# A two-block decoder kernel: square sums and half of the weight sums by accumulating DMA, and weights in order of use

## The chip, the cores and the metric

The kernel runs on one core of one Trainium2 chip. The metric is the device time of one execution in microseconds; the kernel before has a median of 2129.83 us over 3 runs (2126.9 to 2134.0). The engines are TensorE (PE, matrix products), VectorE (DVE), ScalarE (ACT) and GpSimd (POOL); SyncE (SP) issues nearly all DMAs. Each engine works through its own instructions in order and waits for others by semaphores.

## The reference

512 tokens of width 1024 (with 16 more meta tokens in the first block) go through two blocks in fp32. Around the change, each block ends or begins with a feed-forward (FFN) of width 2816:

```python
def rms_norm(x, g):
    y = xf * lax.rsqrt(jnp.mean(xf * xf, axis=-1, keepdims=True) + EPS)
    return y * g
# first block: mixers, then
h = h + m @ w_o
hn = rms_norm(h, norm2_g)
gate, up = jnp.split(hn @ w_gate_up, 2, axis=-1)
x = rms_norm(h + (silu(gate) * up) @ w_down, final_g)
# second block
x = x + 0.5 * swiglu(rms_norm(x, ffn1_norm), ffn1_w_gate, ffn1_w_up, ffn1_w_down)
...   # two attentions with gates g_fox, g_sb
merged = sigmoid(g_fox) * (y_fox @ w_branch_fox) + sigmoid(g_sb) * (y_sb @ w_branch_sb)
x = x + merged @ w_out
x = x + 0.5 * swiglu(rms_norm(x, ffn2_norm), ffn2_w_gate, ffn2_w_up, ffn2_w_down)
x = x + sigmoid(rms_norm(x, ple_norm) @ w_ple_gate) * (p @ w_ple_proj)
```

## The kernel before

Activations lie transposed: 128 features by 512 tokens to a tile, 8 tiles to the width. Every fp32 operand is split into a high part (ACT's cast, `wh`, `zm`, `hh`) and a low part (DVE's difference in `low`, L374), and a product is three matmuls.

In the order of time the stages are: the first block's mixers (to 482 us), its `w_o` (to 527), the first FFN (to 883), the second FFN (to 1267), the second block's mixers (to 1625), its branch product and `w_out` (to 1704), the third FFN (to 2070), and the last gate. At the turn from one to the next stands a *border*: the first is ahead of the first FFN, the second ahead of the second FFN, the third ahead of the third FFN.

An FFN has 22 pairs of 128 gate and 128 up columns, in three parts of 6, 8 and 8 pairs (`CHUNKS`, L1322). A pair is computed by seven products in place of eight (class `Pair`, class `Gated`, `p1` to `p8`), each of 12 matmuls with 256 columns. Its weights come in four pieces `a`, `b`, `c`, `d`; half of piece `a` is a sum of two parts of the up weights (L1113), half of `c` a sum of gate and up parts (L1117), others are differences (L1118, L1120), all on DVE. Each piece is then cast (L1142) and its low half taken. There are 5 buffers for raw pieces and 6 for split ones. After a part's pairs its hidden tiles go through the down weights (`onto`): 8 outputs `o`, in the order 0, 4, 1, 5, 2, 6, 3, 7 (`PAIRED`), each 512 columns wide. `Gated.tail` multiplies gate by the norm factor `rv`, takes silu and multiplies with up; in a down output DVE multiplies by `rv` and scale (L1369) and adds to the residual (L1370), two operations.

Where a stage ends, `normed.post` gets each output. ACT squares it (L940) and POOL adds the square into `ss` (L941); outputs o and o+4 make a quad, whose gains DVE multiplies in (L984, L991), whose three sums POOL takes (L996 to L998, on DVE for the last quad), and which is split into `zm`, the next FFN's operand, by ACT and DVE. So three quads are ready before the last, and the first two pairs start with five products over these three quarters (`early`) before they need the fourth. The mean of the squares is a matmul (L469); `root` computes `rv` with ACT and DVE, and p8 of the first pair cannot start until gate and up of the next are combined behind it (L1292). Ahead of the second FFN there are two statistics (`between`), since the first block's final norm and the next norm are taken together; `rest` then scales the residual by `final_g` (L1439), eight operations among the next pairs.

Inside `ordered()` the order on ACT, DVE and POOL is as recorded. Work beside the products is a task with a planned time: `tick` advances the plan by 358 ns per four-matmul step, and a due task records its next operations then. `feed` lets a task take raw and split buffers in turn and issue the weight loads on SP's queue; `wdma` (L370) is the load.

In the second block, `block2` first loads the residual that was spilled to HBM (L1666, 2 MB), then per output two tiles of gates (L1672, L1673), multiplies, and splits `m` on POOL (L422).

Of the kernel before, what the change touches and what calls it, by code (L numbers as in the profile page):

```python
# [13 lines left out]
S = 512  # L14
# [35 lines left out]
class Net:  # L50
# [3 lines left out]
    def __init__(self, ctx, tc, a):  # L54
# [20 lines left out]
            "ffn": dict(tmp=6, quad=3, x=4, raw2=2, wh2=3, wl2=3, rbc=2, aux=2),  # L75
# [851 lines left out]
    class Stats:  # L927
# [5 lines left out]
        def add(self, x, scale=1.0, eng=None):  # L933
# [12 lines left out]
    def normed(self, gains, more=(), mixed=True):  # L946
# [4 lines left out]
        class Norm:  # L951
# [7 lines left out]
            def post(n, o, x):  # L959
# [9 lines left out]
                elif o < 3:  # L969
                    n.first(o)  # L970
                elif o >= 4:
                    if o == 7:
                        n.first(3)
                    n.second(o - 4, last)
                n.stats[0].add(x)
                for st, f in zip(n.stats[1:], more):
                    st.add(x, f(o))
                if last and mixed:
                    n.task = net.task((n.make or n.root)(), 5500)

            def first(n, k):
                t = net.quad()
                n.mixes.append(t)
                net.nc.vector.tensor_scalar(t[:, 0:2].rearrange("p h c -> p (h c)"), n.res[k], gains(k), None,  # L984
                                            ALU.mult)

            def second(n, k, last):
# [3 lines left out]
                nc.vector.tensor_scalar(b[:, 2:4].rearrange("p h c -> p (h c)"), n.res[k + 4], gains(k + 4), None,  # L991
                                        ALU.mult)

                def sums(eng):
                    t = net.quad()
                    eng.tensor_tensor(t[:, 0:2], b[:, 1:3], b[:, 0:1].broadcast_to([128, 2, HT]), ALU.subtract)  # L996
                    eng.tensor_tensor(t[:, 2], b[:, 2], t[:, 0], ALU.add)  # L997
                    eng.tensor_tensor(t[:, 3], t[:, 2], b[:, 3], ALU.subtract)  # L998
                    return t
                if last:  # L1000
                    nc.scalar.copy(z[:, 0, 0:3], b[:, 1:4])
                    t = sums(nc.vector)
# [5 lines left out]
                def go():  # L1008
                    nc.scalar.copy(z[:, 0, 0:3], b[:, 1:4])
                    t = sums(nc.gpsimd)  # L1010
                    yield 1000
                    net.low(z[:, 1, 0:3], b[:, 1:4], z[:, 0, 0:3])
                    yield 1800
                    nc.scalar.copy(z[:, 0, 3:7], t)
                    yield 1200
# [38 lines left out]
    LAND = 5000  # L1054

    class Tile_:
# [16 lines left out]
        def ready(self, net):  # L1073
            net.fetched(self)
            net.need(lambda: self.ok, *net.splits(self))
            return self.w

        def done(self, net):
            net.leave(self.w)

    class Pair:
# [4 lines left out]
        def __init__(self, one, two):  # L1086
            self.one, self.two = one, two
            self.task, self.t = None, {}

        def fetch(self, net):  # L1090
            def load(to, src, k0):
                net.wdma(to, src[0], src[1], 128, k0, 4)
# [10 lines left out]
            yield from net.take("raw")  # L1103
            self.c = net.get("raw")
# [3 lines left out]
            self.at = net.now  # L1108

        def split_(self, net):  # L1110
            nc = net.nc
            a, x, y = self.a, self.x, self.y
            nc.vector.tensor_tensor(a[:, 4:8], x, y, ALU.add)  # L1113
            yield 700
            yield lambda: self.c is not None
            b, c = self.b, self.c
            nc.vector.tensor_tensor(c[:, 4:8], a[:, 0:4], x, ALU.add)  # L1117
            yield from net.split(self, 0, a, also=lambda: nc.vector.scalar_tensor_tensor(  # L1118
                b[:, 0:4], a[:, 4:8], -1.0, a[:, 0:4], ALU.mult, ALU.subtract))
            yield from net.split(self, 1, b, also=lambda: nc.vector.tensor_tensor(  # L1120
                c[:, 0:4], b[:, 4:8], b[:, 0:4], ALU.subtract))
            yield from net.split(self, 2, c)
            yield lambda: self.d is not None
            yield max(0, self.at + net.LAND - net.now)
            yield from net.split(self, 3, self.d)

        def part(self, net, p):
            net.fetched(self)
            net.need(lambda: p in self.t, *net.splits(self))
            return self.t[p]  # L1130

        def done(self, net, p):
            net.leave(self.t[p])

    def split(self, item, p, raw, single=None, also=None):

        nc = self.nc
        yield lambda: self.items[0] is item
        yield from self.take("w")
        w = self.get("wh", raw.shape[1]), self.get("wl", raw.shape[1])  # L1140
        self.order.append(w)
# [5 lines left out]
        self.give("raw")  # L1147
# [4 lines left out]
        if single or p == 3:  # L1152
            self.items.pop(0)

    def splits(self, item):
        return [x.task for x in self.items[:self.items.index(item) + 1]] + [self.fetch] if item in self.items else []

    def take(self, kind):
        while not self.free[kind]:
            yield lambda: self.free[kind] > 0  # L1160
        self.free[kind] -= 1

    def give(self, kind):
        self.free[kind] += 1

    def leave(self, w):

        self.left.append(w)
        while self.order and any(x is self.order[0] for x in self.left):
            self.order.pop(0)  # L1170
            self.give("w")

    def get(self, tag, nk=KD):

        n = self.WEIGHTS[tag], self.n[tag + "2"]
        self.at[tag] = (self.at.get(tag, -1) + 1) % sum(n)
# [580 lines left out]
```

## Time and profile before

| | |
|---|---|
| median of 3 runs | 2129.83 us (2126.9 to 2134.0) |
| profiled execution | 2130.05 us, span of its trace 2128.1 us |
| mean granted clock of TensorE | 0.979 of full |
| PE / DVE / ACT / POOL busy | 96% / 73% / 48% / 19% |
| DMA | 217.08 MB, 102 GB/s over the span |

Idle time of an engine that is not the bottleneck costs nothing. PE is the busiest, and it is not idle evenly: a table of busy time by stage shows where. At an idle stretch of PE the chain of waits tells what was late: each of its rows is the piece of work that released the next one. "lg L469" is the matmul for a mean, "r", "q" and "s" are the banks of a pair's products, "acc" the outputs of ordinary products. The granted clock is the share of TensorE's full speed (2.4 GHz) that the chip allowed.

### The profile page before, as it was taken

How to read it: one execution, taken by the hardware profiler on the slowest of the kernel's cores; microseconds unless marked ns; L12 is line 12 of the kernel's file. 1: busy time of each engine (PE TensorE's matmuls, PEld its weight loads, DVE VectorE, ACT ScalarE, POOL GpSimd, SP SyncE). 2: the span in 40 equal slices, each digit the busy share in tenths (PEclk: the TensorE clock that was granted, in tenths of full speed). 3: DMA queues.
4: the chain of work that ended last, by engine and by line, in shares of the span. 5: the costliest groups of instructions: out<-in, count | busy, mean ns of one | idle time of the engine just before them, and what ended most of it. 6: DMA issues, size and time to landing. Idle time of an engine off the chain costs nothing.

```text
span 2128.1 us, 30817 instructions
## 1 busy us (share of the span) xinstructions
PE 2032.6 (96%) x11886; PEld 1772.0 (83%) x11886; DVE 1552.1 (73%) x2428; ACT 1022.7 (48%) x1669; POOL 407.3 (19%) x245
## 2 busy tenths in 40 slices
PE   7999999999899999889999999998989989999998
PEld 6788887887889899688989977776777778999987
DVE  5889565547979787897977756666763787977854
ACT  5445554444535345453534537764543453544532
POOL 2333434004000000600000053543333410000010
PEclk9999999999999999889999999999999999999999
DMA  4221222334334435133443432331225534443413
GB/s 114 82 78 45 81 79 80 109 108 135 109 110 129 130 105 149 45 97 112 129 129 100 115 99 81 83 87 45 70 60 183 158 93 121 124 140 91 140 47 90
DMA packets 407459, 217.08 MB, mean 102 GB/s; under 512 B 12166, under 2 KB 402399, under 8 KB 407056
## 3 DMA queue, kind: packets, MB, share of 16 engines
q1 hardware_dynamic: 406670, 214.50, 35.2%
q8 instruction: 93, 1.52, 0.3%
q10 hardware_dynamic: 642, 0.61, 0.1%
q14 instruction: 54, 0.44, 0.1%
HBM read 206.62 MB, written 8.39 MB: 101 GB/s over the span
## 4 chain that ended last, share of the span: by engine, by line
PE 58%; issue 23%; DVE 11%; ACT 4%; POOL 3%; DMA 1%; SPq 0%; DVEq 0%; ACTq 0%; POOLq 0%
PE acc L391 33%; PE r L1235 11%; PE q L1235 5%; PE s L1235 3%; DVE tmp L1579 1%; DVE wl L374 1%; DVE ring L1581 1%; POOL ss L941 1%; PE pv L1606 1%; PE trp L1597 1%; POOL quad L996 1%; ACT wh L357 1%; DMA tmp<-gates 1%; DVE tmp L846 1%; POOL quad L997 0%
## 5 line engine op out<-in xcount | busy, mean ns | idle before, releaser
L1142 ACT CAST wh<-raw 128x1024 fp32r<-128x1024 f32 (+1 forms) x352 | 334.2, 955 | 367.4 <-PE r L1235 144.3
L374 DVE TENSOR_TENSOR wl<-raw,wh 128x1024 fp32r<-128x1024 f32 (+3 forms) x392 | 438.1, 1120 | 79.5 <-ACT wh L1142 40.9
L1235 PE MATMUL r<-zm,wh 128*128 128x256 f32 x2112 | 391.5, 285 | 17.9 <-DVE quad L1292 8.2
L1235 PEld LDWEIGHTS r<-zm,wh 128*128 128x128 f32 x2112 | 329.8, 191 | 22.9 <-DVE quad L1292 9.2
L374 POOL TENSOR_TENSOR wl<-raw,wh 128x1024 fp32r<-128x1024 f32 (+2 forms) x109 | 236.8, 2174 | 399.0 <-ACT wh L357 387.7
L1235 PE MATMUL r<-zm,wl 128*128 128x256 f32 x1056 | 300.3, 284 | 5.7 <-DVE wl L374 5.7
L941 POOL TENSOR_TENSOR ss<-ss,tmp 128x512 f32<-128x512 f32 x42 | 66.8, 1598 | 1173.8 <-ACT tmp L940 1173.8
L391 PE MATMUL acc<-zc,wh 128*128 128x512 f32 (+1 forms) x784 | 264.8, 413 | 5.7 <-DVE tmp L1448 5.6
L357 ACT CAST wh<-raw 128x1024 fp32r<-128x1024 f32 (+2 forms) x149 | 135.7, 911 | 168.0 <-PE acc L391 102.7
L391 PE MATMUL acc<-hh,wh 128*128 128x512 f32 x528 | 208.5, 395 | 0.0
L391 PE MATMUL acc<-hh,wl 128*128 128x512 f32 x528 | 208.5, 395 | 0.0
L391 PE MATMUL acc<-hl,wh 128*128 128x512 f32 x528 | 208.5, 395 | 0.0
L1235 PEld LDWEIGHTS r<-zm,wl 128*128 128x128 f32 x1056 | 202.0, 191 | 6.4 <-DVE wl L374 6.4
L1235 PE MATMUL q<-zm,wh 128*128 128x256 f32 x1056 | 199.8, 287 | 3.4 <-DVE zm L374 2.0
L391 PEld LDWEIGHTS acc<-zc,wh 128*128 128x128 f32 (+1 forms) x784 | 147.2, 192 | 39.9 <-DVE tmp L1448 6.5
L391 PE MATMUL acc<-xl,wh 128*128 128x512 f32 (+1 forms) x496 | 176.5, 356 | 0.0
L391 PE MATMUL acc<-xh,wl 128*128 128x512 f32 (+1 forms) x496 | 176.0, 355 | 0.0
L391 PE MATMUL acc<-xh,wh 128*128 128x512 f32 (+1 forms) x496 | 175.7, 354 | 0.0
L1235 PEld LDWEIGHTS q<-zm,wh 128*128 128x128 f32 x1056 | 165.7, 192 | 5.3 <-DVE zm L374 2.7
L391 PE MATMUL acc<-zc,wl 128*128 128x512 f32 (+1 forms) x392 | 160.9, 410 | 0.0
L1235 PE MATMUL q<-zm,wl 128*128 128x256 f32 x528 | 150.3, 285 | 0.0
L342 ACT ACTIVATE tmp<-tmp 128x512 f32<-128x512 f32 (+3 forms) x196 | 119.2, 609 | 47.5 <-DVE tmp L876 13.3
(347 smaller groups left out, 3901.9 us busy)
## 6 DMA issues: line engine op xcount, KB each, us to landing
raw<-in_w_in_dram SPq DMA_DIRECT2D x91, 512.0 KB
x<-in_ffn_w_up_dram SPq DMA_DIRECT2D x88, 256.0 KB
raw<-in_ffn_w_gate_dram SPq DMA_DIRECT2D x88, 256.0 KB
raw<-in_w_gate_up_dram SPq DMA_DIRECT2D x66, 256.0 KB
raw<-in_ffn_w_down_dram SPq DMA_DIRECT2D x32, 512.0 KB
x<-in_w_gate_up_dram SPq DMA_DIRECT2D x44, 256.0 KB
raw<-in_ffn_w_up_dram SPq DMA_DIRECT2D x44, 256.0 KB
raw<-in_w_down_dram SPq DMA_DIRECT2D x16, 512.0 KB
```

The costliest lines, as they stand in the source:

```text
L342: ins = nc.scalar.activation(out, x, func, **kw)
L357: self.nc.scalar.copy(hi, raw)
L374: (eng or self.nc.vector).tensor_tensor(lo, x, hi.bitcast(F32), ALU.subtract)
L391: nc.tensor.matmul(out, x[:, k], y[:, sl], start=start and i == 0, stop=stop and i == 2)
L846: nc.vector.tensor_tensor(y[:, at + win:], x[:, at + win:], x[:, at:L - win], ALU.add)
L941: (eng or n.nc.gpsimd).tensor_tensor(self.ss, self.ss, q, ALU.add)
L996: eng.tensor_tensor(t[:, 0:2], b[:, 1:3], b[:, 0:1].broadcast_to([128, 2, HT]), ALU.subtract)
L1142: nc.scalar.copy(w[0], raw)
L1235: nc.tensor.matmul(out, x[:, at], y[:, zi], start=first and k == 0 and i == 0, stop=last and k == 3 and i == 2, skip_group_check=True)
L1579: nc.vector.tensor_tensor_scan(c[:, 1:][:, ::-1], c[:, 1:][:, ::-1], self.zero.broadcast_to([128, n - 1]), 1.0, ALU.mult, ALU.add)
L1581: nc.vector.tensor_tensor(b[:, :n - 1], b[:, :n - 1], c[:, 1:], ALU.mult)
L1597: nc.tensor.transpose(tp[:, (i - t) * 128:(i - t + 1) * 128], probs[i][:, t * 128:(t + 1) * 128], self.ident)
```

## The change

1. `wdma` can issue an accumulating DMA on POOL's queue. In 16 of 22 pairs of an FFN (`added`: every second pair, the pair 1, and all of the last part) the sums in `a` and `c` are made by it: the one part is loaded by SP, the other added by POOL's DMA. The loads come in another order, with 2 in place of 4 buffers `x` and 6 in place of 5 raw buffers.
2. Squares are added into `ss` by accumulating DMAs on POOL's queue, the last of a statistic by DVE.
3. In `normed` the gains are multiplied by ACT, the quad's sums taken by DVE. The root task is planned later.
4. In the last part of an FFN the factor `rv` and the scale are multiplied into gate in `tail`, and a down output is one addition.
5. `final_g` multiplies the residual in the first part's down outputs.
6. `p5` of the second pair joins the early products; the pieces of the first two pairs are split in the order of use; buffers are given back one by one.
7. In `block2` the gates of three outputs are loaded first, the residual is loaded behind the first tiles of `w_out`, and DVE splits `m`.

```diff
-    def wdma(self, to, src, c0, cw, k0, nk):
+    def wdma(self, to, src, c0, cw, k0, nk, add=False):
         x = src[k0 * 128:(k0 + nk) * 128, c0:c0 + cw].rearrange("(k p) c -> p k c", p=128)
-        self.nc.sync.dma_start(to, x)
+        if add:
+            self.nc.gpsimd.dma_start(to, x, accum_op=ALU.add)
+        else:
+            self.nc.sync.dma_start(to, x)
...
                 n.nc.scalar.activation(q, x, AF.Square, scale=scale)
-                (eng or n.nc.gpsimd).tensor_tensor(self.ss, self.ss, q, ALU.add)
+                if last:
+                    n.nc.vector.tensor_tensor(self.ss, self.ss, q, ALU.add)
+                else:
+                    def go():
+                        n.nc.gpsimd.dma_start(self.ss, q, accum_op=ALU.add)
+                        yield 0
+                    n.task(go(), 700)
...
-                    n.task = net.task((n.make or n.root)(), 5500)
+                    n.task = net.task((n.make or n.root)(), 8000)
...
-                net.nc.vector.tensor_scalar(t[:, 0:2].rearrange("p h c -> p (h c)"), n.res[k], gains(k), None,
-                                            ALU.mult)
+                net.nc.scalar.mul(t[:, 0:2].rearrange("p h c -> p (h c)"), n.res[k], gains(k))
...
-                    t = sums(nc.gpsimd)
+                    t = sums()
...
             yield from net.take("raw")
-            self.a, self.x, self.y = net.get("raw"), net.own("x", [128, 4, 128]), net.own("x", [128, 4, 128])
-            load(self.x, self.two, 0)
-            load(self.y, self.two, 4)
-            load(self.a[:, 0:4], self.one, 0)
-            self.task = net.task(self.split_(net), net.LAND)
-            self.c, self.d, self.b = None, None, None
+            self.a = net.get("raw")
+            if self.added:
+                load(self.a[:, 4:8], self.two, 0)
+                load(self.a[:, 0:4], self.one, 0)
+                load(self.a[:, 4:8], self.two, 4, True)
...
+            self.task = net.task(self.split_(net), net.LAND + net.ADD * self.added)
+            yield from net.take("raw")
+            self.c = net.get("raw")
+            if self.added:
+                load(self.c[:, 4:8], self.two, 0)
+                load(self.c[:, 4:8], self.one, 0, True)
...
-            nc.vector.tensor_tensor(a[:, 4:8], x, y, ALU.add)
-            yield 700
+            if not self.added:
+                nc.vector.tensor_tensor(a[:, 4:8], self.x, self.y, ALU.add)
+                yield 700
...
+            if self.scale:
+                nc.vector.scalar_tensor_tensor(g, g, self.scale, self.norm.rv, ALU.mult, ALU.mult)
             nc.vector.tensor_tensor(u[:, :HT], self.up, g[:, :HT], ALU.mult)
...
-                    for f in (p.p1, p.p5, p.p2, x.p1, x.p2):
+                    for f in (p.p1, p.p5, p.p2, x.p1, x.p2, x.p5):
                         f(early)
-                    for f in (p.p1, p.p5, x.p1, p.p2, x.p2):
+                    for f in (p.p1, p.p5, x.p1, x.p5, p.p2, x.p2):
                         f((3,))
...
-                t = self.tmp()
-                nc.vector.scalar_tensor_tensor(t, ps, scale, norm.rv, ALU.mult, ALU.mult)
-                nc.vector.tensor_tensor(res[:, o], t, res[:, o], ALU.add)
+                    nc.vector.scalar_tensor_tensor(res[:, o], res[:, o], self.p("final_g", o), norm.rf, ALU.mult,
+                                                   ALU.mult)
+                if c0 + cn < 22:
+                    t = self.tmp()
+                    nc.vector.scalar_tensor_tensor(t, ps, scale, norm.rv, ALU.mult, ALU.mult)
+                    ps = t
+                nc.vector.tensor_tensor(res[:, o], ps, res[:, o], ALU.add)
...
-        res = self.wk.tile([128, 8, S], F32, name="res")
-        nc.sync.dma_start(res, self.spill)
...
+        for _ in range(3):
+            load()
...
-            g, t = self.tmp(), self.tmp()
-            nc.sync.dma_start(g, gates[1, o])
-            nc.sync.dma_start(t, gates[0, o])
+            g, t = loads[o]
...
-            self.split_sb(m[o][0], m[o][1], g, nc.vector if o == 7 else None)
+            self.split_sb(m[o][0], m[o][1], g, nc.vector)
+            load()
...
+            res = self.wk.tile([128, 8, S], F32, name="res")
+            nc.sync.dma_start(res, self.spill)
```

How the order on the engines changes is seen best at the second border. On DVE, the kernel before, from two weight operations ahead of the last output (`acc_8631`) to the operand's last piece (`zm`):

```order
L1113 TENSOR_TENSOR raw2_8597<-x_8598,x_8599 128x512
L374 TENSOR_TENSOR wl2_8634<-raw2_8409,wh2_8633 128x1024
L1369 SCALAR_TENSOR_TENSOR tmp_8665<-acc_8631,rbc_4960 128x512
L1370 TENSOR_TENSOR res_4430<-tmp_8665,res_4430 128x512
L984 TENSOR_SCALAR quad_8668<-res_4430,fg1_384 128x512
L991 TENSOR_SCALAR quad_8668<-res_4430,fg1_384 128x512
L996 TENSOR_TENSOR quad_8673<-quad_8668 128x512
L997 TENSOR_TENSOR quad_8673<-quad_8668,quad_8673 128x256
L998 TENSOR_TENSOR quad_8673<-quad_8673,quad_8668 128x256
L374 TENSOR_TENSOR zm_8670<-quad_8668,zm_8670 128x768
L374 TENSOR_TENSOR zm_8670<-quad_8673,zm_8670 128x1024
```

Two operations stand for the last output's residual, and a weight sum and a weight's low half right ahead of them. The same place after the change (here the last two outputs are `acc_8537` and `acc_8584`):

```order
L1419 TENSOR_TENSOR res_4430<-acc_8537,res_4430 128x512
L377 TENSOR_TENSOR wl_8587<-raw2_8245,wh_8586 128x1024
L1419 TENSOR_TENSOR res_4430<-acc_8584,res_4430 128x512
L999 TENSOR_SCALAR quad_8578<-res_4430,fg1_384 128x512
L1005 TENSOR_TENSOR quad_8625<-quad_8578 128x512
L1006 TENSOR_TENSOR quad_8625<-quad_8578,quad_8625 128x256
L1007 TENSOR_TENSOR quad_8625<-quad_8625,quad_8578 128x256
L377 TENSOR_TENSOR zm_8622<-quad_8578,zm_8622 128x768
L377 TENSOR_TENSOR zm_8622<-quad_8625,zm_8622 128x1024
L945 TENSOR_TENSOR ss_8339<-ss_8339,tmp_8632 128x512
L945 TENSOR_TENSOR ss_8341<-ss_8341,tmp_8635 128x512
```

An output takes one operation, one low half of a weight stands between the last two, and the two additions of squares (L945) follow behind the operand's last piece. On POOL, the kernel before, the last of the second border (`tmp` are squares, `quad` the sums of a quad):

```order
L941 TENSOR_TENSOR ss_8365<-ss_8365,tmp_8574 128x512
L941 TENSOR_TENSOR ss_8367<-ss_8367,tmp_8577 128x512
L996 TENSOR_TENSOR quad_8591<-quad_8529 128x512
L997 TENSOR_TENSOR quad_8591<-quad_8529,quad_8591 128x256
L998 TENSOR_TENSOR quad_8591<-quad_8591,quad_8529 128x256
L941 TENSOR_TENSOR ss_8365<-ss_8365,tmp_8625 128x512
L941 TENSOR_TENSOR ss_8367<-ss_8367,tmp_8628 128x512
L941 TENSOR_TENSOR ss_8365<-ss_8365,tmp_8680 128x512
L941 TENSOR_TENSOR ss_8367<-ss_8367,tmp_8683 128x512
```

After the change the same place on POOL holds only DMAs: square sums (L948) and weight sums (L371).

```order
L371 DMA raw_8364<-in_ffn1_w_up_2_dram 128x4x128
L371 DMA raw2_8383<-in_ffn1_w_gate_2_dram 128x4x128
L948 DMA ss_8339<-tmp_8406 128x512
L948 DMA ss_8341<-tmp_8408 128x512
L948 DMA ss_8339<-tmp_8447 128x512
L948 DMA ss_8341<-tmp_8449 128x512
L948 DMA ss_8339<-tmp_8494 128x512
L948 DMA ss_8341<-tmp_8496 128x512
L948 DMA ss_8339<-tmp_8533 128x512
L948 DMA ss_8341<-tmp_8535 128x512
L948 DMA ss_8339<-tmp_8580 128x512
L948 DMA ss_8341<-tmp_8582 128x512
```

The sums of the quad are gone from POOL, and the DMAs of weights and squares stand in one order.

## Rows read from the trace of the kernel before

**Rows 1.** The page: busy us, share of the span, instructions of an engine.

```profile
PE 2032.6 (96%) x11886; PEld 1772.0 (83%) x11886; DVE 1552.1 (73%) x2428; ACT 1022.7 (48%) x1669; POOL 407.3 (19%) x245
```

**Rows 2.** Stages: us, busy PE, PEld, DVE, ACT, POOL; PEclk, DMA share, GB/s.

```profile
529.00:553.00 24.00, 15.95 (x93) 13.48 (x92) 21.12 (x29) 12.60 (x20) 3.30 (x2) 0.86 0.19 55
553.00:843.00 290.00, 290.00 (x2100) 273.67 (x2099) 238.03 (x359) 136.59 (x204) 0.00 (x0) 1.00 0.45 129
843.00:925.00 82.00, 68.28 (x318) 56.24 (x318) 67.52 (x77) 37.78 (x53) 37.20 (x23) 0.85 0.17 49
...
1625.00:1660.00 35.00, 27.00 (x102) 20.22 (x103) 19.00 (x25) 14.54 (x24) 10.74 (x7) 0.90 0.90 287
...
1707.00:1730.00 23.00, 14.63 (x82) 12.79 (x82) 19.47 (x26) 12.84 (x19) 3.49 (x2) 0.85 0.20 58
```

**Rows 3.** Chain of waits at the second border: start us, us, what.

```profile
886.81 1.97 POOL quad L996
...
893.30 1.77 DVE raw L1113
895.07 2.20 DVE wl L374
...
898.99 0.41 DVE quad L991
...
899.42 0.70 DVE quad L996
900.15 0.43 DVE quad L997
900.61 0.44 DVE quad L998
...
902.78 1.72 POOL ss L941
...
904.55 2.07 PE lg L469 x2
...
908.54 1.16 PE lg L469 x2
...
911.48 1.44 PE q L1235 x12
...
917.80 2.21 PE r L1235 x14
```

**Rows 4.** PE in order of time, first early product at two borders.

```profile
882.50 0.40 PE L1235 MATMUL r<-zm,wh 128*128 128x256 f32 x2
...
1703.43 0.40 PE L1235 MATMUL r<-zm,wh 128*128 128x256 f32 x2
```

**Rows 5.** Chain of waits at the third border.

```profile
1717.22 1.38 PE lg L469 x2
...
1728.98 1.09 PE r L1235 x7
```

**Rows 6.** The page, groups: busy us, mean ns of one, idle before, releaser.

```profile
L1142 ACT CAST wh<-raw 128x1024 fp32r<-128x1024 f32 (+1 forms) x352 | 334.2, 955 | 367.4 <-PE r L1235 144.3
L374 DVE TENSOR_TENSOR wl<-raw,wh 128x1024 fp32r<-128x1024 f32 (+3 forms) x392 | 438.1, 1120 | 79.5 <-ACT wh L1142 40.9
...
L941 POOL TENSOR_TENSOR ss<-ss,tmp 128x512 f32<-128x512 f32 x42 | 66.8, 1598 | 1173.8 <-ACT tmp L940 1173.8
```

**Rows 7.** Line 1117, a weight sum: ns as least/median/most.

```profile
L1117 DVE TENSOR_TENSOR raw<-raw,x x66: 684/692/1670, 499.7 to 1990.4; 128x512 f32<-128x512 f32 x66
```

**Rows 8.** Second block: chain of waits, then what PE waited for.

```profile
1627.31 8.21 DMA tmp<-gates
...
1640.18 3.03 DMA tmp<-gates
...
PE acc L391 <- ACT wh L357: 4.1, 1, 4.1
```

**Rows 9.** PE's waits in the whole run: us, times, longest us.

```profile
PE acc L391 <- DVE tmp L1448: 5.6, 2, 2.8
```

More of the change, by code (lines that the diff above doesn't have):

```diff
@@ L74 @@
     BUFS = {"mix": dict(big=5, mid=6, tmp=10, rbc=1),
-            "ffn": dict(tmp=6, quad=3, x=4, raw2=2, wh2=3, wl2=3, rbc=2, aux=2),
+            "ffn": dict(tmp=6, quad=3, x=2, raw2=3, wh2=3, wl2=3, rbc=2, aux=2),
             "att": dict(big=1, mid=6, tmp=9, rbc=2)}
@@ L931, in __init__, with add @@
             self.net, self.ss = net, None
-        def add(self, x, scale=1.0, eng=None):
+        def add(self, x, scale=1.0, last=False):
             n = self.net
@@ L1102, in fetch @@
             load(self.b[:, 4:8], self.one, 4)
-            yield from net.take("raw")
-            self.c = net.get("raw")
+            self.at = net.now
             yield from net.take("raw")
@@ L1128, in part @@
             net.fetched(self)
-            net.need(lambda: p in self.t, *net.splits(self))
+            net.need(lambda: p in self.t, *net.splits(self, p))
             return self.t[p]
         def done(self, net, p):
-            net.leave(self.t[p])
+            net.give(self.t[p])
     def split(self, item, p, raw, single=None, also=None):
         nc = self.nc
-        yield lambda: self.items[0] is item
+        yield lambda: self.pieces[0] == (item, p)
         yield from self.take("w")
-        w = self.get("wh", raw.shape[1]), self.get("wl", raw.shape[1])
-        self.order.append(w)
+        w = self.get("w", raw.shape[1])
         nc.scalar.copy(w[0], raw)
@@ L1146, in split @@
         self.low(w[1], raw, w[0])
-        self.give("raw")
+        self.give(raw)
         if single:
@@ L1151, in split @@
             item.t[p] = w
[L1152 to L1156, printed above, removed]
-    def take(self, kind):
[L1159 to L1171, printed above, removed]
@@ L1173, in get, with splits @@
-    def get(self, tag, nk=KD):
-        n = self.WEIGHTS[tag], self.n[tag + "2"]
-        self.at[tag] = (self.at.get(tag, -1) + 1) % sum(n)
-        return self.place(tag, nk, more=self.at[tag] >= n[0])
-    def feed(self, items):
-        self.items = list(items)
+        self.pieces.pop(0)
+    def splits(self, item, p):
+        if (item, p) not in self.pieces:
+            return []
+        before = self.pieces[:self.pieces.index((item, p)) + 1]
+        return list(dict.fromkeys(x.task for x, _ in before)) + [self.fetch]
@@ new lines, in open, with get @@
+    def open(self, kind):
+        for q in self.held[kind]:
+            while q and q[0][1]:
+                q.pop(0)
+        return [i for i, (q, n) in enumerate(zip(self.held[kind], self.room[kind])) if len(q) < n]
+    def take(self, kind):
+        while not self.open(kind):
+            yield lambda: bool(self.open(kind))
+    def get(self, kind, nk=KD):
+        i = min(self.open(kind), key=lambda i: len(self.held[kind][i]))
+        if kind == "w":
+            x = self.place("wh", nk, more=i), self.place("wl", nk, more=i)
+        else:
+            x = self.place(kind, nk, more=i)
+        self.held[kind][i].append([x, False])
+        return x
@@ new lines, in give @@
+    def give(self, x):
+        next(t for qs in self.held.values() for q in qs for t in q if t[0] is x)[1] = True
+    def feed(self, items):
+        self.pieces, first = [], None
+        for x in items:
+            if isinstance(x, Net.Tile_):
+                self.pieces.append((x, 0))
+                first = None
+            elif x.lead:
+                first = x
+            elif first:
+                self.pieces += [(first, 0), (first, 1), (x, 0), (x, 1), (first, 2), (first, 3), (x, 2), (x, 3)]
+                first = None
+            else:
+                self.pieces += [(x, p) for p in range(4)]
@@ L1185, in go @@
                 yield from x.fetch(self)
-        self.at, self.order, self.left = {}, [], []
-        self.free = dict(raw=self.WEIGHTS["raw"] + self.n["raw2"], w=self.WEIGHTS["wh"] + self.n["wh2"])
+        self.room = {k: [self.WEIGHTS[t], self.n[t + "2"]] for k, t in (("raw", "raw"), ("w", "wh"))}
+        self.held = {k: [[], []] for k in self.room}
         self.fetch = self.task(go())
@@ L1191, in fetched @@
     def fetched(self, item):
-        self.need(lambda: item.task is not None, self.fetch, *(x.task for x in self.items if x.task))
+        self.need(lambda: item.task is not None, self.fetch, *dict.fromkeys(x.task for x, _ in self.pieces if x.task))
     def tiles(self, src, n, k0=0, nk=KD):
@@ L1337, in ffn @@
             for j in range(cn):
-                x = Net.Gated(self, pairs[j], norm, (hh[:, j], hl[:, j]))
+                x = Net.Gated(self, pairs[j], norm, (hh[:, j], hl[:, j]), scale if c0 + cn == 22 else None)
                 g.append(x)
@@ L1433, in rest @@
             yield 4000
-            rf = self.own("rbc", [128, S])
-            yield from self.root(rf, m1)
-            for o in range(KD):
-                yield 4000
-                x = self.res[:, o]
-                nc.vector.scalar_tensor_tensor(x, x, self.p("final_g", o), rf, ALU.mult, ALU.mult)
+            both.rf = self.own("rbc", [128, S])
+            yield from self.root(both.rf, m1)
         both.wait = self.task(rest())
```

85 lines of the change are left out of this document (51 added, 34 removed).

## The prediction

> **What bounds the kernel now.** I read the page's busy table first, then the busy time by stage, then, in the stages where TensorE is not full, the chain of waits and the waits grouped by releaser. TensorE (PE) is busy 96% of the span [rows 1]. The profiled execution took 2130.05 us against a median of 2129.83, so its span of 2128.1 us and 1.95 us around it stand for the median without correction. By stage [rows 2], the middle of a feed-forward (FFN) keeps PE busy 290.00 of 290 us at a granted clock of 1.00, with VectorE (DVE) at 238.03 and GpSimd (POOL) at nothing: work taken off DVE there is worth nothing. Not full are the three borders, where a projection's last outputs are squared, normed and split before the next FFN can go on: 15.95 of 24 us, 68.28 of 82 and 14.63 of 23, each with a mean clock of 0.85 or 0.86; and the branch product of the second block, 27.00 of 35. The change can win only there, and it can lose in the full stretches.
>
> At the border ahead of the second FFN the chain runs over POOL and DVE [rows 3]: POOL's first sum of a quad (1.97 us), then on DVE, in order, 1.77 and 2.20 us for a weight sum and a weight's low half, then what the last residual needs: its gain, sums of 0.70, 0.43 and 0.44 us, and last POOL's addition of squares, 1.72 us, which releases the mean at 904.55, the second mean at 908.54. PE starts the first early product of the new FFN at 882.50 [rows 4]; product p8 of the first pair, where the irregular part ends, goes on at 917.80 [rows 3], 35.3 us later. The border ahead of the third FFN is the same with one statistic: 1703.43 [rows 4], mean 1717.22, p8 1728.98 [rows 5].
>
> **The change part by part.**
>
> *Square sums, quad sums, gains.* 36 of 42 POOL additions of squares (mean 1.60 us, [rows 6]) become accumulating DMAs; the last of each statistic goes to DVE. The quad sums go from POOL to DVE, 0.70 + 0.43 + 0.44 = 1.57 us a time [rows 3], the gains but the last from DVE to ACT. Where the FFN's last part holds norm factor and scale in its pairs, an output costs DVE one operation and not two; the pairs pay one more, in the full stretch. *Weight sums*: 16 of 22 pairs per FFN, 48 in all, lose two DVE additions of 0.69 us [rows 7] and get two accumulating DMAs of 256 KB each.
>
> For two outputs PE takes 48 matmuls of 512 columns, 10.2 us at a column per cycle of the full 2.4 GHz (256 columns in 0.12 us, [rows 3], agree). At the second border DVE had, for each two, four residual operations of 0.69, two gains of 0.40 [rows 3], a quad's low halves (0.95 and 1.12, the first scaled from 768 of 1024 columns) and two weights with two sums and two low halves (2 x 1.81): 9.3 us by the means. But its operations are slow there: 2.20 us against a mean of 1.12 for a low half, 1.77 against 0.69 for a sum [rows 3, 6, 7], and POOL is busy 37.20 us in that stage, 0.00 in the middle [rows 2]. With a few of those it is over 10.2 and falls behind. After: two residuals (1.4), a quad's sums (1.57) and low halves (2.1), two weights with one sum each (2 x 1.81): 8.7 us, and no tensor operation of POOL beside it, so I take the means. DVE is then on time for the last output; the rows of its order show six operations between that output's residual and the operand's last piece.
>
> *Lead.* Six early products, not five, need only three quarters of the operand: 6 x 9 = 54 matmuls of 256 columns at 0.12 us (12 in 1.44, [rows 3]) = 6.5 us. The last quarter is ready, from its output's end: residual 0.7, gain 0.4, sums 1.57 (ACT's cast of the quad beside them), low halves 0.95 and 1.12, 4.7 us, some 5.5 with the steps between. So PE does not wait. 15 matmuls, 1.8 us, stand ahead of the mean.
>
> Border ahead of the third FFN: mean at 1703.43 + 6.5 + 1.8 = 1711.7, not 1717.22; from mean to p8 I keep the measured 11.8 us (root, factor and combination are the same operations). That is 5.5 us, and 12 more matmuls (p5, 1.4 us) are by then done: **7 us**. The border ahead of the first FFN has the same form and idles as much (8.05 against 8.37 us, [rows 2]): **7 us**. Ahead of the second FFN: first mean 882.50 + 6.5 + 1.8 = 890.8, the second 1.9 us on at 892.7 in place of 908.54, p8 9.3 us behind it as before: 15.8 + 1.4 = **17 us**.
>
> *final_g* moves from a task beside the pairs to the first part's outputs: eight DVE operations in either place, PE full in both; nothing, and if DVE is late at those outputs, up to 8 x 0.7 us.
>
> *Second block.* A load of gates takes 8.21 us behind 2 MB of residual, another 3.03 [rows 8]. After, the gates of three outputs go first and the residual behind six weight tiles. The wait of 4.1 us on a weight [rows 8] goes, the smaller ones there I leave: **4 us**. If the residual, some 8 us from issue to landing, is then later than the first output wants it, the 4 us come back. The wait on L1448, 5.6 us in two [rows 9], stands in part at the border into the mixers, whose sums leave POOL too: 0 to 2.8; I take 0.
>
> **The unknown price and the new waits.** No accumulating DMA is in the trace. Bounds: 3.03 us for 256 KB and 8.21 behind 2 MB [rows 8]; for POOL's own time at the issue, nothing to 1.60 us, its nearest tensor operation [rows 6]. I take 3.03 and nothing, as DMA engines are busy 0.45 in the FFN [rows 2]; added pairs raise 1.25 MB a pair to 1.75, at most some 0.6. The Trainium skill prices a DMA issued by GpSimd at 2.0 us plus its bytes at 436 GB/s (DMA: Bandwidth & Descriptors, "Anatomy of one DMA — SWDGE (gpsimd) path"): an estimate of 2.6 us, by which the sum stays and the margins grow; no row here shows one.
>
> DVE is in order: its last addition of squares waits for the chain of six DMAs into one sum, and the weights' low halves and p8's combination are queued behind it. The DMA that decides is the one before last, issued some 4 us ahead of PE's end; the addition stands 5.5 us behind it. So 9 us are there: 3.03 fits, 8.21 just so.
>
> What the weights tolerate: a pair is 84 matmuls, 10.1 us, in four pieces, so a raw buffer comes free each 2.5 us, and six of them (five before) give one 15 us from issue to release. A plain load takes 3.03 of it, cast and low half 0.96 + 1.12 [rows 6], and about 1.5 pass between them. The accumulating DMA, which must wait for the plain one, has the rest: 8.4 us.
>
> Sum: 7 + 7 + 17 + 4 = 35 us; 2130 - 35 = **2095 us**.
>
> **The rivals.**
>
> *A: the weights come late.* It decides from 8.4 us on: at the upper bounds a DMA costs 8.21 and its own and its fellow's issue 2 x 1.60, 11.4 us, 3 too many. A second sum queues behind the first, a buffer's slack hides some: 1 to 3 us in each of 48 pairs, 48 to 144, less 35 gained: 2143 to 2239, slower. For it: two transfers in series in every pair, the second on a queue that does nothing before. Against: DMA engines half idle, and all rows of 256 KB that are not behind 2 MB stand at 3.03. The Trainium skill has a rule that would bring it about: DVE in a two-port mode locks GpSimd out, so that it cannot write the descriptors of its DMAs (SBUF — State Buffer, "SBUF: two separate sides", the trap that DVE blocks DMA). No row here shows that, and the same page gives additions of two tensors, which most of DVE's work is, no such mode.
>
> *B: one wait for another.* If each DMA into a sum of squares takes the upper bound and the next must wait for it, DVE's last addition, and all behind it, is late by what the mean gained: of the two single borders only p5's 1.4 us each stay, of the double one, with 12 such DMAs on one queue, 0 to 11 of 17. With block two's 4: 7 to 18 us, 2112 to 2123. For it: POOL's queue is in order, and weights' DMAs stand among the squares' in it. Against: an output only comes each 5.1 us.
>
> *C: gained and given back.* Between A and the forecast: 0.6 to 0.8 us lost in each of 48 pairs, 29 to 38 us: 2124 to 2133. For it: PE has no slack at all there [rows 2]. Against: a full stretch mostly stays full or breaks by whole waits.
>
> **How the numbers follow.** Forecast 0.60, from 2082 (with L1448's 2.8, and a clock that falls less: 129 us of borders at 0.85 lack 19 us of full clock, a third of it back is 6; and 4 more in block two, which idles 8) to 2112. B 0.15, C 0.08, A 0.17. 0.3%, 6.4 us, is about what a measurement of this kernel can tell from no change. Faster is the forecast and B, 0.75; same C, 0.08; slower A, 0.17. The range goes from 2076, a little below the best sum (0.04 left out), to 2150, the low end of A (0.13 left out); the forecast's own is 2082 to 2112.
>
> **What would show it.** In the profile after, each border has PE busy without a gap over the six early products, the mean some 8 us behind the first of them (before: 13.8 at the third, 22 and 26 at the second) and p8 about 20 us behind it; DVE's low halves there at 1.1 us, not 2.2; 290 of 290 us in the FFN's middle. A shows as PE idle in the middle, released by the weights' casts behind a DMA; B as DVE idle ahead of its addition of squares, released by a DMA. I am wrong if the middle is under 288 of 290 us, or if the means come less than 3 us earlier.

## The result and the profile after

The changed kernel takes **2107.69 us** (2105.57 to 2110.72, 4 runs), against 2129.74 before: a ratio of **0.9896** (95% interval 0.9874 to 0.9918), 22 us faster. A second set gave 2108.81 and 0.9901 (0.9884 to 0.9919).

The busy table after, the answer to [rows 1]:

```profile
PE 2017.6 (96%) x11886; PEld 1764.4 (84%) x11886; DVE 1462.5 (69%) x2351; ACT 1033.1 (49%) x1690; POOL 446.8 (21%) x301
```

DVE has lost 90 us of work, and the span 20.6. By stage, with the columns of [rows 2]: the first border, an FFN's middle, the second border, the branch product, the third border.

```profile
529.00:553.00 24.00, 16.92 (x118) 15.52 (x117) 14.10 (x21) 10.25 (x17) 1.32 (x1) 0.86 0.31 73
553.00:843.00 290.00, 288.55 (x2074) 271.71 (x2075) 225.14 (x338) 135.93 (x204) 34.93 (x27) 1.00 0.64 151
843.00:920.00 77.00, 68.07 (x368) 59.22 (x367) 54.11 (x80) 47.25 (x67) 18.38 (x19) 0.91 0.64 127
...
1606.00:1640.00 34.00, 33.15 (x142) 26.39 (x142) 25.40 (x36) 18.75 (x28) 0.00 (x0) 1.00 0.92 283
...
1676.00:1712.00 36.00, 21.20 (x133) 19.08 (x132) 17.02 (x25) 12.36 (x18) 6.60 (x6) 0.81 0.40 81
```

The FFN's middle stayed nearly full, the second border and the branch product got better, and the third border got worse: 14.8 of 36 us idle. At the second border DVE's low halves now take 1.23 us each, where the kernel before had 2.20 [rows 3], and only one of them stands ahead of the last output's residual:

```profile
881.57 1.23 DVE L377 TENSOR_TENSOR wl<-raw,wh 128x1024 fp32r<-128x1024 f32 x1 [2.86 <-ACT wh L1164]
882.72 0.68 DVE L1419 TENSOR_TENSOR res<-acc,res 128x512 f32<-128x512 f32 x1
```

Cut at the points that the prediction used (first early product, mean, p8), in us:

| | before | after |
|---|---|---|
| first border: first early product to mean, to p8 | 14.1, 24.9 | 8.3, 21.5 |
| second border: to first mean, second mean, p8 | 22.1, 25.8, 35.3 | 8.7, 10.7, 22.1 |
| third border: to mean, to p8 | 13.8, 25.6 | 16.4, 32.1 |
| branch product and `w_out`, up to the third border | 77.7 | 67.2 |

So the second border gained 13.2 us, the branch product with `w_out` 10.5, the first border 3.4, and the third lost 6.5: together the 20.6 us of the span. The rest nets nothing: the stretches ahead of the first border and behind the second gained 3.0, those behind the first and the third lost 3.0. The longest waits that are left are those for p8, in the whole run (us, times, longest; the 6.9 are at the second border):

```profile
PE r L1274 <- DVE quad L1332: 14.0, 3, 6.9
```

What PE waited for at the third border:

```profile
PE lg L472 <- DVE ss L945: 7.7, 1, 7.7
PE r L1274 <- DVE quad L1332: 3.6, 1, 3.6
PE r L1274 <- ACT quad L1312: 2.0, 1, 2.0
PE q L1274 <- ACT quad L1307: 1.5, 1, 1.5
```

[Rows 5] had the mean 13.8 us behind the first early product. Now the chain of waits of the same place runs through POOL's queue:

```profile
1684.62 0.97 POOL raw L371
...
1686.10 4.54 DMA ss<-tmp
...
1690.73 0.70 DVE ss L945
...
1691.57 2.04 PE lg L472 x2
...
1707.25 2.73 PE r L1274 x11
```

And POOL in order of time there (start, us, line, tile, in brackets the idle time ahead and what ended it):

```profile
1665.34 1.28 POOL L371 DMA_DIRECT2D raw<-in_ffn_w_gate_dram  x1 [3.62 <-DVE res L1741]
1666.09 1.44 POOL L948 DMA_DIRECT2D ss<-tmp  x1
1672.71 0.87 POOL L948 DMA_DIRECT2D ss<-tmp  x1 [5.18 <-ACT zm L1023]
1676.88 0.86 POOL L948 DMA_DIRECT2D ss<-tmp  x1 [3.29 <-ACT tmp L943]
1677.63 1.42 POOL L371 DMA_DIRECT2D raw<-in_ffn_w_up_dram  x1
1681.67 0.88 POOL L948 DMA_DIRECT2D ss<-tmp  x1 [2.62 <-DMA ss<-tmp]
1684.62 1.32 POOL L371 DMA_DIRECT2D raw<-in_ffn_w_gate_dram  x1 [2.06 <-issue]
1686.10 0.89 POOL L948 DMA_DIRECT2D ss<-tmp  x1 [0.16 <-issue]
```

A reader should see three things: weight DMAs (L371) stand among the square DMAs (L948); the last square goes out at 1686.10, directly behind a weight DMA, though the next FFN began at 1675.18; and a square DMA waits for the one before it (1681.67). The last four squares go out 4.2 to 4.8 us apart, about as long as each takes to land, so the chain of squares has a part in the delay too. The price that was open, in KB and median us from issue to landing:

```profile
ss<-tmp POOLq DMA_DIRECT2D x36, 256.0 KB, 3.9
raw<-in_w_gate_up_dram POOLq DMA_DIRECT2D x32, 256.0 KB, 4.9
```

### The profile page after: what moved, and what is told of

Its sections match the earlier page's. It is cut to its first block, busy times and chain, and to the rows that moved or that the text cites. A ratio compares the mean times of both kernels' runs of the same rounds, so it can differ in the third digit from the quotient of the medians.

```text
span 2107.5 us, 31124 instructions
## 1 busy us (share of the span) xinstructions
PE 2017.6 (96%) x11886; PEld 1764.4 (84%) x11886; DVE 1462.5 (69%) x2351; ACT 1033.1 (49%) x1690; POOL 446.8 (21%) x301
## 4 chain that ended last, share of the span: by engine, by line
PE 43%; DVE 7%; ACT 2%; DMA 2%; issue 2%; SPq 0%; POOL 0%; DVEq 0%; ACTq 0%; POOLq 0%
PE acc L394 22%; PE r L1274 11%; PE q L1274 5%; PE s L1274 3%; DVE tmp L1624 1%; DVE ring L1626 1%; PE pv L1651 1%; PE trp L1642 1%; DMA raw<-in_ffn_w_gate_dram 1%; DMA raw<-in_ffn_w_up_dram 0%; DVE wl L377 0%; ACT ring L342 0%; DMA raw<-in_w_out_dram 0%; ACT tmp L342 0%; DMA spill<-res 0%
## 5 line engine op out<-in xcount | busy, mean ns | idle before, releaser
L377 DVE TENSOR_TENSOR wl<-raw,wh 128x1024 fp32r<-128x1024 f32 (+3 forms) x392 | 423.4, 1086 | 92.8 <-ACT wh L1164 57.9
L371 POOL DMA_DIRECT2D raw<-in_ffn_w_up_dram x32 | 41.9, 1308 | 481.1 <-DMA raw<-in_ffn_w_up_dram 176.1
L342 ACT ACTIVATE tmp<-tmp 128x512 f32<-128x512 f32 (+3 forms) x196 | 119.1, 608 | 48.9 <-DVE tmp L879 13.3
```

Source lines behind the costliest of these rows:

```text
L342: ins = nc.scalar.activation(out, x, func, **kw)
L371: self.nc.gpsimd.dma_start(to, x, accum_op=ALU.add)
L377: (eng or self.nc.vector).tensor_tensor(lo, x, hi.bitcast(F32), ALU.subtract)
```

## The experiments

Three undo or move a piece of the change (e2 to e4, with e1 as their control), and two mend what they showed (e5, e6). Of the other six, e7 and e8 put a piece of the kernel before back into e4, and e9 to e12 undo or move one piece of e6. Ratios are to the kernel before, in the same set: e1 to e4, e5 to e8 and e9 to e12 are three sets, in which the kernel before took 2129.46, 2130.97 and 2130.91 us. Differences in us between two sets are of medians, and can be off by the 1.5 us in which these differ.

**e1, the control.** 2108.81 us, 0.9901 (0.9884 to 0.9919); 6.4 us of wait for squares at the third border.

> The changed kernel as it is, as the control of this set: 2107 to 2109 us, with 7.7 us of TensorE's wait for the last addition of squares at the border ahead of the third FFN.

**e2.** DVE makes the weight sums of the first three pairs of each FFN again.

```diff
-            out.append(([Net.Pair((wg, g0 + c), (wu, u0 + c), j % 2 == 0 or c0 + j == 1 or c0 + cn == 22, c0 + j == 0)
+            out.append(([Net.Pair((wg, g0 + c), (wu, u0 + c), (j % 2 == 0 and c0 + j > 2) or c0 + cn == 22, c0 + j == 0)
```

> The weight sums of pairs 0, 1 and 2 of each FFN go back to VectorE, so that no weight DMA stands among the square DMAs in GpSimd's queue at a border. Queue theory (a square's DMA at the third border is issued late because weight DMAs ahead of it in the same in-order queue wait for their raw buffers): the wait of 7.7 us there falls to under 2 us, and the time by 4 to 8 us, to 2100 to 2104. Rival, load theory (the square DMAs are slow because the 2 MB residual and the weights fill the DMA engines to 0.98 in that stage): each square DMA still takes 4.5 us in series and most of the wait, 5 us or more, stays; 2106 to 2112 us.

2103.98 us, 0.988 (0.9862 to 0.9899). The wait for squares is gone from the third border: the last square DMA goes out 5.1 us behind the first early product, not 10.9. A wait of 2.7 us behind a residual is new there (e9 comes back to it). Two of PE's waits there:

```profile
PE r L1274 <- DVE quad L1332: 3.6, 1, 3.6
PE q L1274 <- DVE res L1741: 2.7, 1, 2.7
```

**e3.** The load of the residual stands ahead of the gates' again.

```diff
+        res = self.wk.tile([128, 8, S], F32, name="res")
+        nc.sync.dma_start(res, self.spill)
...
-            res = self.wk.tile([128, 8, S], F32, name="res")
-            nc.sync.dma_start(res, self.spill)
```

> The 2 MB residual of the second block is again loaded at once, ahead of the gates, all else as changed. Load theory: the third border's wait of 7.7 us falls under 3 us, while the branch product's waits come back (5 to 8 us): 2104 to 2112 us. Queue theory: the third border keeps 6 us or more of its wait and the branch product's waits come back on top: 2112 to 2117 us.

2110.66 us, 0.9915 (0.9899 to 0.9932). The wait for squares stays, over the whole run:

```profile
PE lg L472 <- DVE ss L945: 8.4, 2, 8.2
```

So the load of the residual is not the cause of the 7.7 us; with e2, the weight DMAs in POOL's queue are. These also load the DMA engines: in the 20 us up to the third border's start the DMA share was 0.84 in the change, 0.74 in e3 and 0.54 in e2, and a square DMA there landed in 4.3, 4.1 and 3.5 us (medians). With four squares back to back that makes some 3 us of the wait (an estimate: 4 x 0.8 us); the rest is the order. The branch product lost less than either theory said: it takes 71.0 us with `w_out`, in e1 67.1, and the time is within the interval of e1's.

**e4.** No weight sum by DMA.

```diff
-            out.append(([Net.Pair((wg, g0 + c), (wu, u0 + c), j % 2 == 0 or c0 + j == 1 or c0 + cn == 22, c0 + j == 0)
+            out.append(([Net.Pair((wg, g0 + c), (wu, u0 + c), False, c0 + j == 0)
```

> No weight sum by DMA at all: all pairs as the not added ones are now, with two buffers for the parts. Squares stay DMAs. If the weight sums by DMA are what takes the load off VectorE at the borders, the second border loses 3 to 6 us and the time is 2105 to 2115; if what counts there is only GpSimd's tensor operations leaving, the borders stay as they are or gain (the third its 7.7 us) and the time is 2098 to 2103; with the loads waiting for two buffers, pairs may stall, up to 2130 us.

2102.44 us, 0.9875 (0.9857 to 0.9894). It gives DVE 55 us of work back (1517.1 against 1462.5) and is 6 us faster than e1. What remained was the way from the mean to p8: 13.2, 11.4 and 13.3 us at the three borders. ACT and then DVE of e4 at the first border, whose mean starts at 533.93:

```profile
532.70 0.37 ACT L1300 COPY quad<-r 128x256 f32<-128x256 f32 x1 [1.78 <-PE r L1274]
536.66 1.04 ACT L1164 CAST wh<-raw 128x1024 fp32r<-128x1024 f32 x1 [3.59 <-PE r L1274]
537.61 0.36 ACT L1300 COPY quad<-r 128x256 f32<-128x256 f32 x1
```

```profile
538.00 0.42 DVE L1320 TENSOR_TENSOR tmp<-s,quad 128x256 f32<-128x256 f32 x1 [4.46 <-ACT quad L1300]
538.35 1.22 DVE L377 TENSOR_TENSOR wl<-raw,wh 128x1024 fp32r<-128x1024 f32 x1
539.48 0.68 DVE L1052 TENSOR_SCALAR tmp<-lg 128x512 f32<-128x512 f32 x1
```

A cast of weights waits 3.59 us on ACT for PE; a copy stands behind it, on DVE an addition waits 4.46 us for the copy, and behind that stands L1052, the root's first operation: it starts 5.5 us after the mean's matmul. The cast waits because `p5` of the first pair gives back its buffer although p4, recorded later, still reads it. That `p5` was early in the kernel before as well; new are that buffers are given back one by one and that the pieces are cast in another order. No run tells these two apart.

**e5** gives the buffer back when both are recorded:

```diff
             n.nc.scalar.copy(self.u2, self.r)
+            self.both()
+
+        def both(self):
+            self.half = getattr(self, 'half', 0) + 1
+            if self.half == 2:
+                self.w.done(self.net, 1)
...
-                self.w.done(n, 1)
+                self.both()
```

> As e4_no_weight_dmas, but the buffer of the first pairs' piece 1 is given back only when both p4 and p5 are recorded. With p5 early, the change gives it back at p5, and ScalarE's next cast of weights is recorded into that buffer ahead of p4, which still reads it; so ScalarE waits 3.6 us there (measured in e4), and the copies and the root of the norm stand behind it. Theory: this is what made the way from the mean to p8 longer than before (13.2 against 10.8 us at the first border, 11.4 against 9.3 at the second); without it p8 starts 2 to 4 us earlier at each of three borders, and the time falls from 2102 to 2092 to 2098 us. Rival: VectorE's own queue is the limit there (low halves of weights ahead of the root), and the time stays within 2 us of e4.

2091.48 us, 0.9812 (0.9798 to 0.9825): 11 us under e4, at the edge of what was expected. From the mean to p8 it is now 9.5, 9.2 and 10.9 us, 8 of the 9 us by which the two traces differ. ACT no longer waits at that place, and the root starts at 534.17, with the mean at 533.11 (ACT, then DVE):

```profile
532.59 0.37 ACT L1300 COPY quad<-r 128x256 f32<-128x256 f32 x1 [0.35 <-PE r L1274]
533.31 0.37 ACT L1307 COPY quad<-q 128x256 f32<-128x256 f32 x1 [0.35 <-PE q L1274]
```

```profile
534.17 0.69 DVE L1052 TENSOR_SCALAR tmp<-lg 128x512 f32<-128x512 f32 x1 [0.74 <-PE lg L472]
```

**e6** also records the root without its planned pauses (`yield 900`, `600` and `between`'s second `1000` become 0).

> As e5, and the root's operations on VectorE and ScalarE are recorded right behind the mean, without the planned pauses between them. Theory (the root stands behind weights' casts and low halves in in-order queues): 1 to 3 us more at each border, 2088 to 2095 us. Rival: only e5's release counts, and this stays within 2 us of e5, or loses since copies that TensorE waits for now stand behind the root.

**2086.86 us, 0.9794 (0.9781 to 0.9808)**, the best version: 43 us under the kernel before and 21 under the change. PE's waits for p8 in the whole run fell from 12.8 us in e4, and as many in e5, to

```profile
PE r L1274 <- DVE quad L1338: 9.6, 3, 3.5
```

But PE waits longer for ACT's copies ahead of it (3.2 us, 1.6 in e5), and from the first early product to p8 the three borders take 18.5, 20.9 and 23.8 us, in e5 17.8, 20.5 and 24.9: no less in sum. The intervals of the two overlap, so it is not shown that the pauses of the root cost anything.

**e7** (on e4). POOL takes the quad's sums again, all but the last quad's, and two planned pauses are again those of the kernel before.

```diff
-                    t = sums()
+                    t = sums(nc.gpsimd)
...
-                    yield 1000
+                    yield 1800
...
-                    yield 1300
+                    yield 1200
```

> As e4_no_weight_dmas, but the three sums of a quad (but the last one's) are taken by GpSimd again, as in the kernel before. If GpSimd's tensor operations beside VectorE's are what made the borders long, VectorE's operations at the second border are slow again (near 2 us for a low half) and the time rises by 5 to 12 us over e4, to 2107 to 2114. Rival: VectorE's count of operations counts, not their slowness; then taking 1.57 us a quad off VectorE leaves the time within 2 us of e4 or lowers it. GpSimd's queue also holds the square DMAs, which wait behind the sums: up to 4 us a border.

2121.83 us, 0.9954 (0.9941 to 0.9966): 19 us over e4, more than expected. DVE, in e7's second border:

```profile
879.28 1.23 DVE L377 TENSOR_TENSOR zm<-quad,zm 128x1024 fp32r<-128x1024 f32 x1 [2.53 <-ACT zm L1023]
...
887.80 2.02 DVE L377 TENSOR_TENSOR zm<-quad,zm 128x768 fp32r<-128x768 f32 x1
```

One is a wait for ACT's cast of POOL's sums, one an operation that takes 0.95 us undisturbed (the mean of its twelve in e4; 1.31 in e7) and 2.02 while POOL's sums run. Waits of the first kind come to 11.7 us in the run, the twelve operations of this form to 4.3 over e4: it is as much that POOL is late as that it disturbs.

**e8** (on e4). POOL adds the squares by tensor operations again.

```diff
-                    def go():
-                        n.nc.gpsimd.dma_start(self.ss, q, accum_op=ALU.add)
-                        yield 0
-                    n.task(go(), 700)
+                    n.nc.gpsimd.tensor_tensor(self.ss, self.ss, q, ALU.add)
```

> As e4_no_weight_dmas, but the squares are added by GpSimd's tensor additions again (the last of a statistic by VectorE). If GpSimd's tensor operations beside VectorE's count, the second border, with 12 of them, loses 4 to 10 us: 2106 to 2112. Rival: an addition of 1.6 us on GpSimd is early enough and disturbs little, and the time stays within 2 us of e4, so that the square DMAs bring nothing either.

2114.55 us, 0.9921 (0.9909 to 0.9934): 12 us over e4, so the square DMAs are worth that. Its chain at the second border, while POOL adds from 881.00 to 883.7 and from 889.15 to 891.7:

```profile
881.10 1.51 DVE quad L1003
...
882.63 1.37 DVE quad L1004
...
890.59 2.17 DVE wl L377
...
894.64 0.43 DVE quad L1003
...
895.10 0.44 DVE quad L1004
```

The last two rows are the same quad sums with POOL at rest: 0.43 and 0.44 us. Over the run the mean of the twelve L1003 is 1.02 us, in e4 0.43.

**e9** (on e6) fetches the residual ahead of `w_out`'s third tile.

```diff
+            res = self.wk.tile([128, 8, S], F32, name="res")
+            fetch = wo[2].fetch
+
+            def fetch_after_res(net):
+                nc.sync.dma_start(res, self.spill)
+                yield from fetch(net)
+            wo[2].fetch = fetch_after_res
...
-            res = self.wk.tile([128, 8, S], F32, name="res")
-            nc.sync.dma_start(res, self.spill)
```

> As e6_release_and_root, but the residual of the second block is loaded ahead of the third tile of w_out and not behind the sixth. In e6 VectorE waits 4.4 us for that load, and runs late from there to the third border, where TensorE waits 2.7 us behind a residual. Theory: both waits go, 2082 to 2086 us against 2087. Rival: the tiles of w_out, now behind 2 MB, are late by as much, and the time stays or rises to 2092 us.

2090.43 us (2086.1 to 2091.88), 0.9812 (0.9794 to 0.9829): not told apart from e6. DVE's wait of 4.4 us for the residual went, but PE's wait at the third border did not, so its cause is not that load:

```profile
PE q L1274 <- DVE res L1752: 2.7, 1, 2.7
```

The other runs show where it comes from. It stands, at 2.7 us, in e2, e4, e5, e6, e9, e11 and e12, where DVE makes the first pairs' weight sums, and in none of the change, e1, e3 and e10, where DMAs make them. In e6 the last residual starts 7.4 us behind the first early product, in the change 2.9; on DVE a weight sum (L1138) stands right ahead of it, and others earlier:

```profile
1670.59 1.22 DVE L377 TENSOR_TENSOR wl<-raw,wh 128x1024 fp32r<-128x1024 f32 x1 [2.25 <-ACT wh L1164]
1671.73 0.68 DVE L1138 TENSOR_TENSOR raw<-raw,x 128x512 f32<-128x512 f32 x1
1672.34 0.68 DVE L1747 TENSOR_TENSOR res<-acc,res 128x512 f32<-128x512 f32 x1
```

**e10** (e6 with the weight DMAs of the change).

> As e6_release_and_root, but with the weight sums by accumulating DMA in 16 of 22 pairs, as in the change: the change itself with the buffer's release and the root mended. If these DMAs cost by the third border alone (squares behind them in GpSimd's queue) this is 4 to 9 us slower than e6, 2091 to 2096 us, with a wait for squares of 4 to 8 us at the third border. Rival: with the borders shorter, the relief of VectorE counts, and it is within 2 us of e6 or faster.

2095.66 us, 0.9839 (0.9822 to 0.9856): 9 us over e6. At its third border PE waits for squares again, and not for the residual:

```profile
PE lg L472 <- DVE ss L945: 6.5, 1, 6.5
```

That border takes 26.8 us from the first early product to p8, in e6 23.8: 3 of the 9 us. Of the others, 4 lie between the second border's p8 and the branch product (704.6 us, 700.5 in e6). That stretch takes 699 to 708 us in the traces of these runs, so they can't be put down to a cause.

**e11** (on e6): two operations to a last-part output again, `scale` not in the pairs.

> As e6_release_and_root, but in the last part of an FFN a down output takes two operations of VectorE again (scale and factor, then the addition), and the pairs have none more. If VectorE's count at the second border matters, eight operations of 0.69 us more make it late again there: 2 to 6 us, 2089 to 2093 us. Rival: VectorE has the time, and it is within 2 us of e6.

2096.94 us, 0.9845 (0.9826 to 0.9864): 10 us over e6, more than expected. At the second border, the means and p8 come 5.1 us later behind the first early product, which is within what was expected, and PE waits for an output's first operation:

```profile
PE q L1274 <- DVE tmp L1423: 3.4, 1, 3.4
```

Another 4 us lie in the stretch ahead of the branch product (704.9 us) and are not explained.

**e12** (on e6): `x.p5` out of both early lists.

> As e6_release_and_root, but with five early products and not six (p5 of the second pair in its old place). Theory of the prediction: at the double border the operand's last quarter needs all six, and p5 is also done for nothing while waiting: 1.1 to 2 us lost at each of three borders, 2090 to 2093 us. Rival: TensorE then waits as long as before and does p5 later in a gap it has anyway (3 us at p8): within 2 us of e6.

2095.04 us, 0.9835 (0.9818 to 0.9851): 8 us over e6. At the second border PE waits 5.0 us for p8, not 3.5, and the mean comes 11.8 us behind the first early product, not 9.3.

## Why the prediction was right, and where its terms were not

The forecast was 2095 us, faster, in a range of its own from 2082 to 2112; it came 22 and not 35 us faster. That the time lies in the range is in part luck: the third border lost 6.5 us where 7 were to be gained, and the second block's 10.5 us for 4 made up half of that. With 4 there the time would have been some 2114 us, where rival B stood. Point by point:

1. *Lead and mean: right at two borders, wrong at the third.* Forecast 8.3 us from the first early product to the mean, measured 8.3 and 8.7 at the first two. At the third 16.4: there the means came 2.6 us later, by the prediction's own sign ("less than 3 us earlier") the mark of being wrong. The step that failed is "The DMA that decides is the one before last, issued some 4 us ahead of PE's end" and, on it, "So 9 us are there: 3.03 fits, 8.21 just so". It priced one DMA landing and left out its place in POOL's queue. A square DMA lands in 3.9 us (median), but it went out 11 us after the next FFN had begun, behind a weight DMA and behind the square DMA before it. That is what rival B had for it, at one border instead of three, and by the order more than by B's price of 8.21 us a DMA (e2, e3).
2. *"From mean to p8 I keep the measured 11.8 us": failed.* It became 13.2 for 10.8 at the first border, 11.4 for 9.5 at the second, 15.7 for 11.8 at the third. The operations are the same, their order is not: p5 gave back a buffer that p4 still read, and ACT's cast into it held up copies and root (e4, e5). I had counted operations and not looked at what now stood ahead of them on ACT.
3. *Second border: right in kind, 13.2 + 1.4 for 17.* The kinds of edit that carry it are told apart by e7, e8 and e11, in the versions they start from: quad sums off POOL 19 us, squares off POOL 12, one operation an output 10, over the whole run (5 of them at the second border). The 48 pairs' sums by DMA relieve DVE too, which spares PE the 2.7 us at the third border (e9), but cost more than that (e4, e10). One sum of this part was off: by the row cited for it, 256 columns in 0.12 us, two outputs take PE 11.5 us and not 10.2, so by its means DVE had 2 us to spare, and it took slow operations to make it late.
4. *Second block: mis-sized, 10.5 for 4.* I counted one wait of 4.1 us. The smaller ones went too (PE 33.15 of 34 us), and so did the low clock: a mean of 0.90 in [rows 2], 1.00 after. The residual's place brings 4 of it (e3); gates first and `m` split by DVE share the rest, untested one by one.
5. *Weight sums.* The price was inside its bounds, 4.7 to 4.9 us for 3.03 to 8.21, POOL's time at the issue 1.3 us for 0 to 1.6, and the middle stayed at 288.55 of 290: rival A did not come, as six buffers with 8.4 us to spare had it. The forecast took the lower bounds, 3.03 and nothing, and both were too low. The argument that all loads of 256 KB not behind 2 MB stood at 3.03 was a misreading: in the chain of [rows 8], between its rows, a load of a `w_branch_sb` tile took 4.17 us. I credited them as part of DVE's relief, and in sum they are a loss: 9 us in the mended version, 6 in the change.
6. The slow DVE operations beside POOL's: shown by e7 and e8 (2.02 us for 0.95, 1.51 for 0.43), and by the low halves at the second border, forecast at 1.1 us and not 2.2, measured at 1.23.

What stays open: how the delay of the squares divides between the weight DMAs ahead of them and their own chain, the 4 us of e10 and e11 that lie outside the borders, and `final_g`'s new place and the root's later plan, which no run tests alone.

## What to carry to other kernels

A DMA queue of an in-order engine is a resource like the engine: before moving urgent transfers there, list what stands ahead of them and what each of those waits for. Where products are recorded in a new order, look at the release of what they read: it belongs behind the last reader, or the next writer waits on an engine that others need. Work taken off an engine is worth what its critical stretch gains: 55 us less on DVE, nearly all in full stretches, came with 6 us lost (by what replaced them), and eight operations at a border gave 5 us there and 10 in all.

## What the hardware showed that was not expected

An accumulating DMA of 256 KB took a median of 3.9 us from SBUF to SBUF and 4.7 to 4.9 from HBM, where the DMA share was 0.64 in the FFN's middle, and held POOL 0.86 us at its issue for a square, 1.30 for a weight (medians). At the second border PE's waits between the first early product and p8 shrank from 13.7 to 7.1 us, and the mean granted clock there rose from 0.71 to 0.91, so that gaps closed gave back more than their length: the stretch is 13.2 us shorter.
